# A decoder trunk on one core: the last expert's down products follow the ones ahead in two pieces, and a branch gets a hint

## The chip, the core and the metric

The kernel runs on one core of a Trainium2 chip. TensorE (PE in the profile) multiplies, VectorE (DVE) and ScalarE (ACT) work element by element, GpSimd (POOL) does a little beside them, and SyncE (SP) issues the loads. The metric is the device time of one execution in microseconds, the median of three runs. A trace of one further execution shows when every instruction ran.

## The reference

Two decoder layers over 256 tokens of width 1024, in float32. Layer 0 mixes with a retention, layer 1 with a sparse attention whose keys and values come from the stream after layer 0. Both end with the same kind of mixture of experts, which is all that the change touches:

```python
for l in range(DEPTH):                       # 2 layers
    mix = retention(...) if l < 1 else nsa_attention(...)
    h = layer_norm(ALPHA * h + mix, ...)
    h = layer_norm(ALPHA * h + moe(h, ...), ...)

def moe(x, ...):                             # 256 tokens, 16 experts in 4 groups, each token has 2
    y = zeros_like(x)
    for e in range(16):
        he = (silu(x @ w_gate[e]) * (x @ w_up[e])) @ w_down[e]   # 1024 -> 512 -> 1024
        y = y + w[:, e:e + 1] * he
    return y
```

## The kernel before

Each expert takes up to 64 tokens: a gather by a one-hot product writes them into a tile `xT` (three buffers, two experts in each), and all products of the expert run on these 64 rows. If some expert has more than 64 tokens, a loop behind a branch (`overflow`, L880) does the rest; with these inputs it isn't entered, and all engines jump past it. Every engine loads the largest count from memory, compares and branches. On the way past it the engine adds to its own counter what the loop would have added, once its work ahead is done; engines that wait for such a counter wait for that.

TensorE's work for expert e stands in this order. `gate_up(e + 1)` makes 16 product pairs from 64 rows; in the middle of it, behind the fourth weight step, stand the transposes of expert e (`turn`, L804), the scatter of expert e - 1 (L825, four products of 128x512 into the sums `y_moe`) and other small pieces. Then `down(e)` makes the 64x512 products of expert e into two PSUM banks, one for each half of the 1024 outputs, on two halves of TensorE's columns (`both`, L776). Between them stand the other engines: `hidden` takes the bank of `gate_up` to the rows `sh` (ScalarE's Silu at L795, VectorE's multiplication at L796), `turn` goes from `sh` over a bank to `hT` (ScalarE, L805), and `hilo` takes the banks of `down` to `out` as a rounded high part (ScalarE, L222) and the rest (VectorE, L223). For the last expert there is no `gate_up` to hide this in: transposes, scatter of expert 14, `down(15)` and scatter of expert 15 follow each other.

The weights come in chunks of 1 MB through a ring, loaded by SyncE in their order; an expert has six (four for gate and up, two for down). The expert weights are used as they are. The dense weights that come behind layer 0's experts are split first, by half chunks, into a high part (ScalarE, L114) and a low part (VectorE, L115), into four places `st`. `Weights.ahead` splits as far as places and a limit allow; `get` gives the next half chunk and lets go of those before, `take` lets go of none. Before, two half chunks are split at expert 14 and two at expert 15 of layer 0 (`split_ahead`). The order of all instructions is that of the code, engine by engine; the framework adds the waits.

Behind the experts come the statistics of the sums (L306), and the normalisation, in layer 0 (`next_rows`) into transposed columns `hTh` and `hTl` (L1020, L1026), in layer 1 (`last_rows`) into the output.

Of the kernel before, what the change touches and what calls it, by code (L numbers as in the profile page):

```python
# [10 lines left out]
F32 = mybir.dt.float32  # L11
F32R = mybir.dt.float32r
# [7 lines left out]
P = 128  # L20
# [3 lines left out]
NE = 16  # L24
# [129 lines left out]
class Trunk:  # L154
# [46 lines left out]
    def alloc(self, name, side="right"):  # L201

        self.extra.append(self.tc.alloc_tile_pool(name=name, bufs=1, side=side, reuse_waits="tile"))
        return self.extra[-1]

    def split_ahead(self, n):

        self.W.limit = 2 * self.moe_end(0) + n
        self.W.ahead()

    def first_place(self, l, side):

# [501 lines left out]
    def experts(self, pool, keep, oh0, rest, hh, hl, y, l):  # L714
# [4 lines left out]
        out = []  # L719
# [31 lines left out]
        def weigh(g):  # L751

            b = self.bank()
            for i in range(4):
                for tb in range(2):
                    nc.tensor.matmul(b[0:64, i:i + 1], oh[g][:, tb, i, :].bitcast(F32),
                                     self.w[:, tb, 4 * g + i:4 * g + i + 1], start=(tb == 0), stop=(tb == 1))
            ws[g] = pool.tile([P, 4], F32, tag="wsl", name=f"wsl{l}_{g}", bufs=2)
            nc.vector.tensor_copy(ws[g][0:64], b[0:64, 0:4])
# [12 lines left out]
        def both(x, w, b, first, last, o=0):  # L772

            for i in range(2):
                c = slice(64 * i ^ o, (64 * i ^ o) + 64)
                nc.tensor.matmul(b[i][c, :], x, w[:, i, :], start=first, stop=last)  # L776

        def gate_up(e, fill, at=3):


            b = self.bank()
            for k in range(8):
                both(xT[e // 2][:, e % 2, k, :], self.W.get(2)[0], [b, b], k == 0, k == 7, 64)
                if k == at:
                    for f in fill:
                        f()
            return b
# [10 lines left out]
        def hidden(e, b):  # L798
            gated(b, ws[e // 4][0:64, e % 4:e % 4 + 1])

        def turn(hT):
            b = self.bank()
            for k in range(4):
                nc.tensor.transpose(b[:, k * P:k * P + P], rows[:, k * P:k * P + P], self.ident)  # L804
            nc.scalar.copy(hT, b.rearrange("p (k s) -> p k s", k=4)[:, :, 0:64])  # L805

        def down(e, hT):

            b = [self.bank(), self.bank()]
            for k in range(4):  # L810
                both(hT[:, k, :], self.W.get(2)[0], b, k == 0, k == 3)
            if not out:
                out.append(self.first.tile([P, 2048], F32R, tag="raw", name=f"out{l}"))
            d = []
            for i in range(2):
                t = out[0][:, i * 512:i * 512 + 512]
                hi, lo = t[64 * i:64 * i + 64], t[64 - 64 * i:128 - 64 * i]
                self.hilo(hi, lo, b[i][64 * i:64 * i + 64, :])
                d.append(t)
            return d  # L820

        def scatter(e, d, last):

            o = oT[e // 4][:, e % 2, e % 4 // 2]
            return [lambda tb=tb, nh=nh: nc.tensor.matmul(y[tb][nh], o[:, tb, :], d[nh], start=(e == 0), stop=last)  # L825
                    for nh in range(2) for tb in range(2)]
# [40 lines left out]
        def overflow():  # L867
# [8 lines left out]
            d = part[0:64, 256:512]  # L876
            pe = pool.tile([P, 2, 2], F32, name=f"o_pe{l}")
            wsl = pool.tile([P, 1], F32, name=f"o_ws{l}")
            most = nc.values_load(self.cnt[0:1, 0:1], min_val=0, max_val=2 * P)
            with self.tc.If(most > 64), self.tc.For_i(0, NE, 1) as e:  # L880
                nc.vector.tensor_copy(pe[:, 0, :], self.pos[:, :, ds(e, 1)])
                nc.vector.tensor_copy(pe[:, 1, :], self.w[:, :, ds(e, 1)])

# [45 lines left out]
        hidden(0, b)  # L929
        d = self.gb = None  # L930
        picks, todo, more = [], [], alpha()
        for e in range(NE):
            g = e // 4 + 1
            if e % 4 == 1 and g < 4:
                oh[g] = self.one_hot(keep, g, l)
                picks = gather(g)
            hT = pool.tile([P, 4, 64], F32, tag="hT", name=f"hT{l}_{e}", bufs=1)
            fill = [lambda: turn(hT)] + (scatter(e - 1, d, False) if e else [])
            if e % 4 == 0 and e:
                fill.append(lambda: turn_hot(e // 4))  # L940
            if e + 1 < NE:
                fill += more[:1] + picks[:2] + todo[:2]
                more, picks, todo = more[1:], picks[2:], todo[2:]
                b = gate_up(e + 1, fill)
                if e % 4 == 2 and g < 4:
                    weigh(g)
                hidden(e + 1, b)
            else:
                for f in fill:
                    f()  # L950
            if e == 13:
                overflow()
            if l == 0 and e >= NE - 2:
                self.split_ahead(2 * (e - NE + 3))
            d = down(e, hT)
            if e == 0:
                turn_hot(0)
            if l == 1 and e > 9 and self.gb is None and self.W.slots:
                todo += norm_rows()
        for f in todo:  # L960
            f()
        self.ready(AF.Sqrt)
        for f in scatter(NE - 1, d, True):
            f()
        self.W.limit = 2 * len(self.W.srcs)

# [607 lines left out]
```

## Time and profile before

| what | value |
|---|---|
| median of 3 runs | 890.33 us (889.71 to 890.62) |
| the profiled execution | 891.96 us, its span 890.10 us |
| TensorE busy | 846.9 us, 95% of the span |
| VectorE, ScalarE busy | 405.6 us, 339.7 us |
| 1024 gate and up products 128x512 (L776) | 233.9 us busy |
| 512 down products 128x512 (L776) | 118.6 us busy |
| branches in the executed path | 2, one in each layer, at L880 |

TensorE is busy in nearly every slice of the span. A matmul of the code on float32 data is two in the trace, so `down` has sixteen and `gate_up` thirty-two; two run at a time on the two halves of the columns. In a timeline row, "x16" are sixteen instructions merged, and what stands in brackets is the idle time of that engine ahead of the row and what ended it.

### The profile page before, as it was taken

The page shows a single profiled execution, that of the slowest core. Times are in us where ns is not written, and L with a number is a line of the kernel's source. Part 1 is how long each engine was busy: PE and PEld are TensorE (multiplying, and loading weights), DVE is VectorE, ACT ScalarE, POOL GpSimd, SP SyncE. Part 2 cuts the span into 40 slices and gives each one's busy share as a digit, 9 for nine tenths or more (in the row PEclk, how much of TensorE's full clock was granted, in tenths as well). Part 3 has the DMA queues.
Part 4 walks back from the last instruction along what each step waited for, and adds up shares of the span by engine and source line. Part 5 has one row for each costly group of instructions (what it writes and reads, how often), then busy time and mean ns, then how long its engine had stood idle before and what let it go on. Part 6 is the DMA issues. An engine that isn't in the chain of part 4 may idle for free. (4 is left out here: it accounts for less than half of the span.)

```text
span 890.1 us, 12109 instructions
## 1 busy us (share of the span) xinstructions
PE 846.9 (95%) x4738; PEld 535.0 (60%) x4738; DVE 405.6 (46%) x817; ACT 339.7 (38%) x657; POOL 50.0 (6%) x70
## 2 busy tenths in 40 slices
PE   7999999998999999999879998999999999999993
PEld 5998989886545454453338786666744545445431
DVE  4666776864422132221077877775433222222215
ACT  4335344434332331322164455785523233232312
POOL 1000000000200000000000004220110000000001
PEclk8999999999999999999999999899999999999997
DMA  9966354578699999999943456205779999999801
GB/s 332 426 248 231 119 218 142 190 279 350 224 409 410 426 423 427 422 425 423 365 156 138 169 230 237 96 1 203 308 280 388 425 427 424 427 426 427 375 3 47
DMA packets 37283, 259.83 MB, mean 292 GB/s; under 512 B 4217, under 2 KB 4401, under 8 KB 6369
## 3 DMA queue, kind: packets, MB, share of 16 engines
q1 hardware_dynamic: 36432, 255.87, 71.3%
q0 software_dynamic: 640, 2.97, 1.0%
q8 instruction: 42, 0.69, 0.3%
q14 instruction: 25, 0.20, 0.1%
q10 hardware_dynamic: 144, 0.11, 0.0%
HBM read 257.88 MB, written 1.05 MB: 291 GB/s over the span
## 5 line engine op out<-in xcount | busy, mean ns | idle before, releaser
L776 PE MATMUL bank<-raw,xT 128*64 128x512 f32 x1024 | 233.9, 596 | 0.8 <-ACT xT L735 0.8
L776 PEld LDWEIGHTS bank<-raw,xT 128*64 128x64 f32 x1024 | 76.7, 137 | 125.9 <-issue 118.5
L115 DVE TENSOR_TENSOR st<-raw,st 128x1024 fp32r<-128x1024 f32 x92 | 111.4, 1234 | 55.4 <-ACT st L114 55.3
L114 ACT CAST st<-raw 128x1024 fp32r<-128x1024 f32 x92 | 94.5, 1048 | 80.4 <-PE bank L339 32.4
L776 PE MATMUL bank<-raw,hT 128*64 128x512 f32 x512 | 118.6, 601 | 5.2 <-PEq L880 3.3
L323 PE MATMUL bank<-xh,st 128*128 128x256 f32 x512 | 93.6, 284 | 3.0 <-ACT st L114 2.5
L223 DVE TENSOR_TENSOR out<-bank,out 64x512 fp32r<-64x512 f32 x64 | 44.1, 689 | 96.7 <-ACT out L222 95.6
L776 PEld LDWEIGHTS bank<-raw,hT 128*64 128x64 f32 x512 | 40.5, 138 | 73.3 <-issue 70.1
L323 PEld LDWEIGHTS bank<-xh,st 128*128 128x128 f32 x512 | 80.4, 192 | 3.6 <-ACT st L114 2.7
L222 ACT CAST out<-bank 64x512 fp32r<-64x512 f32 x64 | 37.1, 579 | 104.6 <-PE bank L776 103.8
L323 PE MATMUL bank<-xl,st 128*128 128x256 f32 x256 | 72.3, 283 | 0.0
L796 DVE SCALAR_TENSOR_TENSOR sh<-bank,wsl,sh 64x512 f32<-64x512 f32 x32 | 23.7, 741 | 105.3 <-ACT sh L795 105.1
L795 ACT ACTIVATE sh<-bank 64x512 f32<-64x512 f32 x32 | 19.0, 593 | 94.9 <-PE bank L776 94.9
L323 PEld LDWEIGHTS bank<-xl,st 128*128 128x128 f32 x256 | 49.6, 194 | 0.1
L805 ACT COPY hT<-bank 128x256 f32<-128x256 f32 x32 | 11.9, 373 | 86.9 <-PE bank L804 86.9
L356 PE MATMUL acc<-st,gh 128*128 128x512 f32 x128 | 42.9, 407 | 1.8 <-DVE st L115 1.1
L339 PE MATMUL bank<-st,hTh 128*128 128x512 f32 x128 | 42.2, 401 | 1.7 <-DVE nt L1022 1.4
L825 PE MATMUL y_moe<-out 128*128 128x512 f32 x128 | 38.6, 419 | 4.4 <-DVE out L223 4.4
L840 DVE SCALAR_TENSOR_TENSOR al<-bank,wsm,al 128x256 f32<-128x256 f32 x16 | 7.7, 484 | 72.0 <-ACT al L839 72.0
L339 PE MATMUL bank<-st,xh 128*128 128x512 f32 x128 | 40.5, 393 | 0.0
L733 DVE TENSOR_SCALAR xT<-bank,wsm 128x128 f32<-128x128 f32 x64 | 21.9, 404 | 34.0 <-PE bank L727 24.2
L735 ACT ACTIVATE xT<-bank,wsm 128x128 f32<-128x128 f32 x64 | 24.1, 456 | 19.3 <-PE bank L727 19.3
(328 smaller groups left out, 1205.4 us busy)
## 6 DMA issues: line engine op xcount, KB each, us to landing
raw<-in_w_moe_dram SPq DMA_DIRECT2D x190, 1024.0 KB, 10.3
raw<-in_w_dense_dram SPq DMA_DIRECT2D x49, 1024.0 KB, 7.0
raw<-in_w_moe_dram SPq DMA_DIRECT2D x4, 512.0 KB, 15.6
xT<-in_x_T_dram SPq DMA_DIRECT2D x4, 256.0 KB, 5.4
raw<-in_w_dense_dram SPq DMA_DIRECT2D x2, 512.0 KB, 10.0
rt<-in_c_ret_dram POOLq DMA_DIRECT2D x1, 1024.0 KB, 11.1
gb<-in_ln_rows_dram POOLq DMA_DIRECT2D x1, 1024.0 KB, 6.9
out_dram<-lf_n SPq DMA_DIRECT2D x4, 256.0 KB, 2.0
```

What stands on the lines that cost most here:

```text
L114: self.nc.scalar.copy(hi, r)
L115: (eng or self.nc.vector).tensor_sub(lo, r, hi.bitcast(F32))
L222: self.nc.scalar.copy(hi, src)
L223: self.nc.vector.tensor_sub(lo, src, hi.bitcast(F32))
L323: self.nc.tensor.matmul(b[:, m, :], w[:, kk, c], x[:, k, :], start=(k == 0 and i == 0 and m == 0), stop=(k == 7 and i == 2 and m == 1))
L339: self.nc.tensor.matmul(b[tb], x[:, k, c], w[:, kk, :], start=(k == 0 and i == 0), stop=(k == 7 and i == 2))
L356: self.nc.tensor.matmul(y[tb][nh], x[a][:, c], w[b][:, 0, n], start=False, stop=last and i == 2)
L733: nc.vector.tensor_scalar(t, v, c, d, op0=ALU.mult, op1=ALU.add)
L735: nc.scalar.activation(t, v, AF.Identity, bias=d, scale=c)
L776: nc.tensor.matmul(b[i][c, :], x, w[:, i, :], start=first, stop=last)
L796: nc.vector.scalar_tensor_tensor(rows[0:64], b[0:64], w, rows[0:64], op0=ALU.mult, op1=ALU.mult)
L825: return [lambda tb=tb, nh=nh: nc.tensor.matmul(y[tb][nh], o[:, tb, :], d[nh], start=(e == 0), stop=last) for nh in range(2) for tb in ran ...
```

## The change

There are three parts. (1) `down` gets the tile that it writes, a number of pieces, and work that is put behind its second weight step. At expert 14 that work is expert 15's `turn`, into a tile of its own (`hT_last`, in a buffer of `xT`). Expert 15's `down` then follows expert 14's at once, in two pieces of 256 of the 512 columns of each bank, with its own result tile `d_last`, and both scatters stand behind it. (2) `mark_branch_hint_location` puts one hint instruction into TensorE's stream, for the branch past the overflow. (3) Layer 0's splits ahead move: three half chunks at expert 13, just behind the branch, in place of two at expert 14 and two at expert 15; the fourth follows in `next_rows`, at a call of `ahead` that was there before.

```diff
-    def split_ahead(self, n):
-
-        self.W.limit = 2 * self.moe_end(0) + n
-        self.W.ahead()
...
-        def down(e, hT):
+        def down(hT, t, parts=1, fill=()):
+
 
             b = [self.bank(), self.bank()]
-            for k in range(4):
-                both(hT[:, k, :], self.W.get(2)[0], b, k == 0, k == 3)
...
+            ws = []
+            n = 512 // parts
+            for p in range(parts):
+                c = slice(p * n, p * n + n)
+                for k in range(4):
+                    if k == 2 and p == 0:
+                        for f in fill:
+                            f()
+                    if p == 0:
+                        ws.append(self.W.take(2)[0] if k and parts > 1 else self.W.get(2)[0])
+                    both(hT[:, k, :], ws[k][:, :, c], [v[:, c] for v in b], k == 0, k == 3)
+                for i in range(2):
+                    v = t[:, i * 512 + c.start:i * 512 + c.stop]
+                    self.hilo(v[64 * i:64 * i + 64], v[64 - 64 * i:128 - 64 * i], b[i][64 * i:64 * i + 64, c])
+            return [t[:, i * 512:i * 512 + 512] for i in range(2)]
...
+            self.tc.mark_branch_hint_location(f"past{l}", "LikelyTaken", engines=(mybir.EngineType.PE,))
             most = nc.values_load(self.cnt[0:1, 0:1], min_val=0, max_val=2 * P)
-            with self.tc.If(most > 64), self.tc.For_i(0, NE, 1) as e:
+            with self.tc.If(most > 64, label=f"past{l}"), self.tc.For_i(0, NE, 1) as e:
...
-        for e in range(NE):
+        spare = lambda dtype, name: pool.tile([P, 1024], dtype, tag="xT", name=f"{name}{l}", bufs=3)
+        for e in range(NE - 1):
...
             if e == 13:
                 overflow()
-            if l == 0 and e >= NE - 2:
-                self.split_ahead(2 * (e - NE + 3))
-            d = down(e, hT)
+                if l == 0:
+
+                    self.W.limit = 2 * self.moe_end(0) + 3
+                    self.W.ahead()
...
+            between = []
+            if e == NE - 2:
+
+                last = spare(F32, "hT_last")[:, 0:256].rearrange("p (k s) -> p k s", k=4)
+                between.append(lambda: turn(last))
+            d = down(hT, out[0], 1, between)
...
+        d_last = down(last, spare(F32R, "d_last"), 2)
+        for f in scatter(NE - 2, d, False):
+            f()
         self.ready(AF.Sqrt)
-        for f in scatter(NE - 1, d, True):
+        for f in scatter(NE - 1, d_last, True):
             f()
```

The lines of the changed kernel have other numbers: `both` is L771, `turn` L799, `hilo` L217 and L218, the branch L881. On TensorE, at the end of layer 1's experts, this stood before (`bank375` and `bank376` take expert 14's products, `bank378` and `bank379` expert 15's, `raw239` and `raw240` are weight chunks; in brackets the engines whose counters the row waits for):

```order
L776 MATMUL bank376_7346<-raw239_6855,hT1_14_7311 64x512
L804 MATMUL bank377_7360<-cst_105,sh1_5762 128x128 [waits DVE_49]
L804 MATMUL bank377_7360<-cst_105,sh1_5762 128x128 x3
L825 MATMUL y_moe1_00_5752<-out1_5925 128x512 [waits DVE_49]
L825 MATMUL y_moe1_10_5754<-out1_5925 128x512
L825 MATMUL y_moe1_01_5753<-out1_5925 128x512 [waits DVE_49]
L825 MATMUL y_moe1_11_5755<-out1_5925 128x512
L776 MATMUL bank378_7370<-raw240_6861,hT1_15_7359 64x512 [waits DMAHW7_49,Activation_49]
L776 MATMUL bank379_7371<-raw240_6861,hT1_15_7359 64x512 [waits PE_49]
L776 MATMUL bank378_7370<-raw240_6861,hT1_15_7359 64x512
```

With the change, from the last of expert 14's products on, it reads:

```order
L771 MATMUL bank376_7362<-raw239_6869,hT1_14_7326 64x512
L771 MATMUL bank378_7382<-raw240_6875,hT_last1_7360 64x256 [waits DMAHW7_49,Activation_49]
L771 MATMUL bank379_7383<-raw240_6875,hT_last1_7360 64x256 [waits PE_49]
L771 MATMUL bank378_7382<-raw240_6875,hT_last1_7360 64x256
L771 MATMUL bank379_7383<-raw240_6875,hT_last1_7360 64x256
L771 MATMUL bank378_7382<-raw241_6906,hT_last1_7360 64x256 [waits DMAHW0_49]
L771 MATMUL bank379_7383<-raw241_6906,hT_last1_7360 64x256
L771 MATMUL bank378_7382<-raw241_6906,hT_last1_7360 64x256 [waits DMAHW1_49]
L771 MATMUL bank379_7383<-raw241_6906,hT_last1_7360 64x256
L771 MATMUL bank378_7382<-raw240_6875,hT_last1_7360 64x256 [waits DVE_49]
L771 MATMUL bank379_7383<-raw240_6875,hT_last1_7360 64x256 [waits DVE_49]
L771 MATMUL bank378_7382<-raw240_6875,hT_last1_7360 64x256
```

Expert 15's products now follow expert 14's; the transposes into `bank377` went up between the two halves of expert 14's products, and both scatters stand behind the second piece, which begins at the two rows that wait for VectorE. Layer 0 has the same order.

On ScalarE, just behind layer 0's branch (the first row), this stood before (`st256` to `st259` are split half chunks of the dense chunks `raw128` and `raw129`; `bank162` and `bank163` hold expert 13's products):

```order
L880 UNCONDITIONAL_BRANCH x2
L222 CAST out0_2353<-bank162_3711 64x512
L222 CAST out0_2353<-bank163_3712 64x512
L805 COPY hT0_14_3729<-bank165_3743 128x256
L795 ACTIVATE sh0_2194<-bank164_3730 64x512
L114 CAST st256_3763<-raw128_3339 128x1024
L114 CAST st257_3766<-raw128_3339 128x1024
L222 CAST out0_2353<-bank166_3769 64x512
L222 CAST out0_2353<-bank167_3770 64x512
L805 COPY hT0_15_3783<-bank168_3784 128x256
L114 CAST st258_3794<-raw129_3355 128x1024
L114 CAST st259_3797<-raw129_3355 128x1024
```

and with the change:

```order
L881 UNCONDITIONAL_BRANCH x2
L114 CAST st256_3712<-raw128_3339 128x1024
L114 CAST st257_3715<-raw128_3339 128x1024
L114 CAST st258_3718<-raw129_3355 128x1024
L217 CAST out0_2341<-bank162_3721 64x512
L217 CAST out0_2341<-bank163_3722 64x512
L800 COPY hT0_14_3739<-bank165_3753 128x256
L790 ACTIVATE sh0_2194<-bank164_3740 64x512
L800 COPY hT_last0_3773<-bank168_3780 128x256
L217 CAST out0_2341<-bank166_3774 64x512
L217 CAST out0_2341<-bank167_3775 64x512
L217 CAST d_last0_3794<-bank169_3795 64x256
```

Three casts went ahead of expert 13's, and no split is left between the casts of the last experts; VectorE's subtractions moved alike. On TensorE the hint for layer 0's branch is the second instruction of the program, and that for layer 1's stands where the loop's code has been passed in layer 0, ahead of expert 13's down products:

```order
L881 COMPARE_AND_BRANCH
L881 UNCONDITIONAL_BRANCH x2
L1581 BRANCH_PREFETCH_HINT
L771 MATMUL bank162_3721<-raw118_3184,hT0_13_3333 64x512
L771 MATMUL bank163_3722<-raw118_3184,hT0_13_3333 64x512
```

The hint is new there; the rows around it stood so before.

## Rows read from the trace of the kernel before

**Rows 1.** Timeline of TensorE's products around layer 0's branch: start, length, instructions, [idle before]

```profile
424.40 3.65 PE L776 MATMUL bank<-raw,xT 128*64 128x512 f32 x16
...
431.33 4.89 PE L776 MATMUL bank<-raw,hT 128*64 128x512 f32 x13 [3.27 <-PEq L880]
436.41 0.65 PE L776 MATMUL bank<-raw,hT 128*64 128x512 f32 x2 [0.20 <-issue]
436.84 0.59 PE L776 MATMUL bank<-raw,xT 128*64 128x512 f32 x1
```

**Rows 2.** Instructions of the branch, layer 0: ns min/median/max, first and last start

```profile
L880 PEldq COMPARE_BRANCH  x1: 5888/5888/5888, 425.0 to 425.0; - x1
...
L880 DVEq EVENT_SEMAPHORE  x1: 21/21/21, 430.0 to 430.0; - x1
```

**Rows 3.** Stretches: length, busy time of each engine, granted clock, DMA share, GB/s

```profile
431.54:434.96 3.42, 3.42 (x10) 1.21 (x8) 0.00 (x0) 0.00 (x0) 0.59 (x2) 0.50 0.85 350
...
552.21:555.13 2.92, 0.00 (x1) 0.01 (x2) 2.78 (x6) 1.06 (x5) 2.84 (x4) 0.88 0.55 233
555.20:558.00 2.80, 2.80 (x12) 1.72 (x12) 2.77 (x8) 2.35 (x7) 2.65 (x4) 0.50 0.00 0
...
851.92:855.40 3.48, 3.48 (x17) 1.43 (x19) 0.00 (x0) 0.00 (x0) 0.00 (x0) 1.00 0.00 0
```

**Rows 4.** Instructions of the branch, layer 1

```profile
L880 PEldq COMPARE_BRANCH  x1: 3632/3632/3632, 847.0 to 847.0; - x1
...
L880 DVEq EVENT_SEMAPHORE  x1: 21/21/21, 851.7 to 851.7; - x1
```

**Rows 5.** Timeline of all engines, first products behind layer 1's branch

```profile
851.92 3.65 PE L776 MATMUL bank<-raw,hT 128*64 128x512 f32 x16 [1.73 <-DVEq L880]
```

**Rows 6.** Timeline of TensorE at the end of layer 1's experts

```profile
865.00 3.60 PE L776 MATMUL bank<-raw,hT 128*64 128x512 f32 x16
868.53 0.66 PE L804 MATMUL bank<-cst,sh 128*128 128x128 f32 x4
869.99 1.46 PE L825 MATMUL y_moe<-out 128*128 128x512 f32 x4 [0.80 <-DVE out L223]
871.37 3.65 PE L776 MATMUL bank<-raw,hT 128*64 128x512 f32 x16
876.41 1.46 PE L825 MATMUL y_moe<-out 128*128 128x512 f32 x4 [1.38 <-DVE out L223]
```

**Rows 7.** Timeline of TensorE at the end of layer 0's experts

```profile
445.85 3.60 PE L776 MATMUL bank<-raw,hT 128*64 128x512 f32 x16
...
457.26 1.46 PE L825 MATMUL y_moe<-out 128*128 128x512 f32 x4 [1.38 <-DVE out L223]
```

**Rows 8.** Timeline of VectorE at the end of layer 1's experts

```profile
865.84 0.74 DVE L796 SCALAR_TENSOR_TENSOR sh<-bank,wsl,sh 64x512 f32<-64x512 f32 x1 [8.24 <-ACT sh L795]
...
875.67 1.41 DVE L223 TENSOR_TENSOR out<-bank,out 64x512 fp32r<-64x512 f32 x2 [5.01 <-ACT out L222]
877.11 1.89 DVE L306 BATCH_NORM_STATS2 lf_st<-y_moe 128x6 f32<-128x512 f32 x3
```

**Rows 9.** Timeline of all engines among layer 0's experts

```profile
384.49 0.37 ACT L805 COPY hT<-bank 128x256 f32<-128x256 f32 x1 [2.89 <-PE bank L804]
...
385.16 0.40 PE L727 MATMUL bank<-oh,hh 128*128 128x256 f32 x2
...
386.80 0.40 PE L727 MATMUL bank<-oh,hl0l 128*128 128x256 f32 x2
...
390.62 0.98 PE L756 MATMUL bank<-w,oh 128*64 128x1 f32 x15
```

**Rows 10.** Groups on VectorE, 452 to 480: busy us, mean ns | idle

```profile
L115 DVE TENSOR_TENSOR st<-raw,st 128x1024 fp32r<-128x1024 f32 x5 | 6.0, 1223 | 2.7 <-ACT st L114 2.7
...
L1026 DVE TENSOR_TENSOR hTl<-nt,hTh 128x256 fp32r<-128x256 f32 x2 | 0.9, 426 | 0.1
```

**Rows 11.** The one load of a dense chunk issued at 423.0: time to landing

```profile
DMA to landing us min/median/max: 8.3/8.3/8.3
```

More of the change, by code (lines that the diff above doesn't have):

```diff
@@ L805, in turn @@
             nc.scalar.copy(hT, b.rearrange("p (k s) -> p k s", k=4)[:, :, 0:64])
-        def down(e, hT):
+        def down(hT, t, parts=1, fill=()):
             b = [self.bank(), self.bank()]
-            for k in range(4):
-                both(hT[:, k, :], self.W.get(2)[0], b, k == 0, k == 3)
[L812 to L820, printed above, removed]
+            ws = []
[13 more added lines that the diff above has]
+            return [t[:, i * 512:i * 512 + 512] for i in range(2)]
         def scatter(e, d, last):
@@ L942, in experts @@
                 fill += more[:1] + picks[:2] + todo[:2]
[L943 to L950, printed above, removed]
+            more, picks, todo = more[1:], picks[2:], todo[2:]
+            b = gate_up(e + 1, fill)
+            if e % 4 == 2 and g < 4:
+                weigh(g)
+            hidden(e + 1, b)
             if e == 13:
                 overflow()
-            if l == 0 and e >= NE - 2:
-                self.split_ahead(2 * (e - NE + 3))
-            d = down(e, hT)
+                if l == 0:
+                    self.W.limit = 2 * self.moe_end(0) + 3
+                    self.W.ahead()
+            if e == 0:
+                out.append(self.first.tile([P, 2048], F32R, tag="raw", name=f"out{l}"))
+            between = []
[3 more added lines that the diff above has]
+            d = down(hT, out[0], 1, between)
             if e == 0:
```

## The prediction

> **What bounds the kernel now.** I read the page first, then the waits at the branch, then the last expert of each layer, since the diff touches nothing else. TensorE is busy nearly throughout, so only stretches where it stands still or runs at half clock can give time back. The reader is to see three of them, all on TensorE, all on the path because the engines around it have nothing else to finish.
>
> First, the branch around the overflow in layer 0. The products of expert 14's gate and up end at 424.40 + 3.65 = 428.05, and the first product behind the branch starts at 431.33 [rows 1]: 3.27 us idle, put down to TensorE's own branch. That branch stood 5.89 us in TensorE's sequencer, from 425.0 to 430.9, while VectorE had posted its count at 430.0 [rows 2]. TensorE needs that count, since VectorE makes the rows `sh` just ahead of its own branch. Behind the wait come slow products: 16 of them take from 431.33 to 436.84, 5.51 us [rows 1], where the same 16 in layer 1 take 851.92 to 855.38. The granted clock was 0.50 (1.2 GHz) from 431.54 to 434.96 [rows 3], which makes 1.7 us of the 2.05 lost; the rest is a stop that the row at 436.41 calls "issue" [rows 1].
>
> Second, the same branch in layer 1. TensorE's branch took 3.63 us from 847.0, so it was through at 850.6, and VectorE's count came only at 851.7 [rows 4]; the products start at 851.92 after 1.73 us, released by VectorE [rows 5]. The clock stayed at 1.00 behind it [rows 3].
>
> Third, the end of each layer's experts. From the start of expert 14's down products (865.00) to the first scatter of expert 15 (876.41) it takes 11.41 us [rows 6], the same in layer 0 (445.85 to 457.26) [rows 7]. In it TensorE idles 0.80 us until VectorE has the low part of expert 14, and 1.38 us until it has that of expert 15 [rows 6].
>
> **The tail, worked out.** Write T for 865.00. The products come in pairs, sixteen in about 3.43 us. Expert 15's transposes move between the two halves of expert 14's down products: they want `sh`, which VectorE finishes at 865.84 + 0.74, T + 1.58 [rows 8], and TensorE gets there at T + 1.8, so they wait for nothing. Four transposes hold TensorE about 0.42 us beside their drain [rows 6], so expert 15's products can start at S = T + 4.0 instead of T + 6.37. ScalarE copies `hT_last` (0.37 us [rows 9]) long before.
>
> The first piece is sixteen products of 256 columns. No row has that shape in half-width tiles. At half of 3.43 it is 1.72 us; at the pace of the 128x256 gather products, two each 0.235 us (385.16 to 386.80 is seven such steps [rows 9]), 1.88 us. I take 1.72 and keep 1.88.
>
> Now the point that the diff hides: the second piece's first two products carry a wait on VectorE each, since both pieces lie in the same two PSUM banks. The pieces do not overlap with their own evacuation. The results of piece one can be read at S + 1.93. ScalarE's cast of 64x256 costs near the 0.37 of a 128x256 copy; VectorE's subtraction 0.42, as the 128x256 one of 426 ns [rows 10], where 64x512 takes 0.69 (1.41 for two [rows 8]). Bank one: cast until S + 2.33, subtraction until S + 2.78. Bank two: subtraction until S + 3.21. With 0.06 us to TensorE the second piece runs in full from S + 3.27, to S + 4.99. Expert 14's scatter, put behind it, takes some 1.1 us and covers the last casts (0.16 + 0.37 + 0.42 and three handovers, S + 6.06). Expert 15's scatter so starts at S + 6.1 = T + 10.1, against T + 11.41: 1.3 us less. The bank statistics start 0.70 us behind it now, at 877.11, because VectorE is still at L223 until 877.07 [rows 8]; then it is free, which gives another 0.1. So 1.4 us per layer, 2.8 us in all. Bounds: with 1.88 us pieces 1.1; with the subtraction at the full 0.69 as well 0.4; nothing above 1.5. The activation table load moves with the last cast and is done well before the square root.
>
> **The branch hint.** It is one instruction at the start of the block, per layer; ahead of the first products and inside a wait it costs nothing. If the code behind the branch is there when TensorE arrives, layer 0 is held by VectorE's count as layer 1 is: 430.0 + 0.22 (851.7 to 851.92) is 430.2, so 1.1 us less. The stop of 0.34 us at 436.4 should be more code that arrives late, since TensorE comes to the target 5 us earlier; I take 0.3 (0 to 0.34). The half clock I leave: idle falls from 3.27 to 2.2 us; 1.73 us left the clock at 1.00 in layer 1 [rows 3, 5], 2.92 us ahead of 555.13 left it at 0.50 [rows 3]; 2.2 lies between. Layer 1 gains nothing: there VectorE is later than the branch already.
>
> The Trainium skill, Runtime: NRT & Kernel Launch, section "Instruction fetch mechanics", says that a taken branch out of the fetched pages forces a DMA fetch, and that prefetch is purely sequential. The rows of 5.89 and 3.63 us agree with the first. By the second the hint would change nothing, and the sum would be the tail's 2.8 us alone; no row here shows a hinted branch.
>
> **Three half chunks split ahead.** In layer 0 three casts and three subtractions (1.22 us each on VectorE [rows 10], and I take no more for a cast) move from the tail to just behind the branch, ahead of expert 13's casts in ScalarE's and VectorE's queues. What stands behind them there are those casts and the scatter of expert 13, which waits for them. The third needs the second dense chunk, which is issued at 423.0 and lands 8.3 us later, at 431.3 [rows 11], so ScalarE is through by 432.5 and VectorE by 433.8; expert 13's products end at 433.7 at the earliest, and VectorE's turn comes only behind a cast. Cost nothing; cover gone only if the chunk lands later than 433. The fourth half chunk goes into the normalisation of layer 0, between the third and last pair of transposed columns: bounded by 0 and one 1.22 us step; I take 0, as 36 products of the same projection come before its first use. SP's next loads (the ring place of the first dense chunk) start earlier by some 2 us and one later chunk starts later; the ring stays ahead. The tail has no split left in ScalarE's queue, but its split casts cost nothing there before either.
>
> **Rivals.** *B, the clock comes back too:* with 2.2 us idle the stretch at 0.50 may not come; 1.7 us more. For it: 1.73 us did no harm. Against it: 2.92 us did. 890.33 - 5.9 = 884.4. *C, the hint does nothing:* TensorE's prefetch takes no notice or the target is displaced in the 400 us between hint and branch. For it: the hint stands far ahead, and the rule above. Against it: nothing in the rows. 890.33 - 2.8 = 887.5. *D, slower:* products of 256 columns pay the price of 512, because each brings its own weight load; 32 loads instead of 16 in expert 15's down products. Then each layer loses 3.43 and gains 1.4: with the hint 890.33 + 4.1 - 1.4 = 893.0. It turns the whole slower once one such product occupies more than 0.173 us (2 x (1.4 - 32 x (s - 0.107)) + 1.4 = 0). Against it: fifteen products of one column with their 64-wide loads go through in 0.98 us, 0.065 each [rows 9], and the gather's 256 columns go at 0.117. *E, no change to speak of:* no hint effect and VectorE's half subtraction as long as the whole one: 0.4 per layer, 889.5.
>
> **How the numbers follow.** The sum is 2.8 + 1.1 + 0.3 = 4.2 us. The profiled execution took 891.96 (span 890.10 and 1.86 around it), 1.63 over the median 890.33; I take the difference from the median: 886.1. Chances: this forecast (A) 0.40, B 0.19, C 0.25, D 0.06, E 0.10. The range reaches from B with the tail at its upper bound (884.0) to C with 1.0 per layer (888.4), and holds A, B and nearly all of C. Within 0.2% is 1.8 us to either side, about what a measurement of this kernel can tell from no change: A, B and C are faster (0.84), E is the same (0.10), D slower (0.06).
>
> **What would show it.** In the new trace: TensorE's branch in layer 0 under 1 us, the idle before expert 13's down products near 2.2 us and released by VectorE; in layer 1 still 1.7. From expert 14's down products to expert 15's scatter 10.0 us in both layers, with an idle of about 1 us between the two pieces, released by VectorE at the split line. It is wrong if the second piece starts without that wait (then 1.2 us more per layer), if the branch still takes 5 us, or if products of 256 columns come less than twice as often as those of 512.

## The result

The changed kernel takes 885.47 us (median of 17 runs, 882.87 to 888.73) where the kernel before took 890.62 on the same chip (17 runs, 888.96 to 894.12): 0.9938 of the time, 95% interval 0.9926 to 0.9951, or 4.4 to 6.6 us less. The forecast said 886.1, within 884.0 to 888.4. Of the experiments below, one run of e2 (1239.2 us at a mean granted clock of 0.648) and one of e4 (903.5 us at 0.933) stand far above the others of their kernel, and the medians and ratios leave them out.

The profiled execution of the changed kernel took 886.01 us (span 884.0). The first thing to look at is TensorE at the branch in layer 0 (start, length, then the work, and in brackets the idle time before it; [rows 1] before):

```profile
424.61 3.65 PE L771 MATMUL bank<-raw,xT 128*64 128x512 f32 x16
430.43 3.65 PE L771 MATMUL bank<-raw,hT 128*64 128x512 f32 x16 [2.17 <-ACT st L114]
433.88 3.63 PE L771 MATMUL bank<-raw,xT 128*64 128x512 f32 x16
```

Three things have gone: 1.10 us of the idle time (3.27 to 2.17), the slow pace of the sixteen products behind it (3.45 us to the next ones, where 5.51 passed before), and the stop that cut them in two at 436.41. The stop cost more than its 0.20 us of idle time, because it left the products behind it out of step: the last of the sixteen ran beside the first of expert 15's gate products, and the transposes behind those came only at 440.85 (TensorE, before):

```profile
436.90 0.59 PE L776 MATMUL bank<-raw,hT 128*64 128x512 f32 x1
437.27 3.65 PE L776 MATMUL bank<-raw,xT 128*64 128x512 f32 x15
440.85 0.66 PE L804 MATMUL bank<-cst,sh 128*128 128x128 f32 x4
```

From the first of the sixteen to these transposes it took 9.52 us; now it takes 7.01 (430.43 to 437.44). The releaser in the bracket is the profile's guess. The instructions of the branch in this stretch show the real one ([rows 2] before):

```profile
L881 PEldq COMPARE_BRANCH  x1: 388/388/388, 425.2 to 425.2; - x1
...
L881 DVEq COMPARE_BRANCH  x1: 72/72/72, 429.6 to 429.6; - x1
L881 DVEq EVENT_SEMAPHORE  x1: 21/21/21, 430.2 to 430.2; - x1
```

TensorE's branch took 0.39 us instead of 5.89, and what is waited for now is VectorE's count at 430.2, with the products 0.2 us behind it. In layer 1 the branch fell from 3.63 to 0.35 us and nothing came of it, since VectorE's count was the later one there already ([rows 4, 5] before):

```profile
L881 PEldq COMPARE_BRANCH  x1: 350/350/350, 842.2 to 842.2; - x1
...
L881 DVEq EVENT_SEMAPHORE  x1: 21/21/21, 846.8 to 846.8; - x1
```

```profile
847.11 3.65 PE L771 MATMUL bank<-raw,hT 128*64 128x512 f32 x16 [1.73 <-DVEq L881]
```

The second thing is the granted clock, in the row of stretches (length; busy time of the engines; clock; DMA share; GB/s). Before, most of the products behind the branch ran at 0.50 [rows 3]; now, over the idle time and over the products:

```profile
428.26:430.43 2.17, 0.01 (x2) 0.03 (x1) 0.81 (x2) 1.86 (x3) 0.11 (x1) 1.00 1.02 408
430.43:433.88 3.45, 3.45 (x16) 1.40 (x18) 3.45 (x3) 1.78 (x2) 0.90 (x2) 1.00 1.01 399
```

The third is the end of layer 0's experts ([rows 7] before, and [rows 6] for the same in layer 1). TensorE:

```profile
442.45 1.89 PE L771 MATMUL bank<-raw,hT 128*64 128x512 f32 x8
444.26 0.66 PE L799 MATMUL bank<-cst,sh 128*128 128x128 f32 x4
444.85 1.94 PE L771 MATMUL bank<-raw,hT 128*64 128x512 f32 x8
446.62 1.90 PE L771 MATMUL bank<-raw,hT_last 128*64 128x256 f32 x16
449.41 2.40 PE L771 MATMUL bank<-raw,hT_last 128*64 128x256 f32 x16 [0.90 <-DVE d_last L218]
451.74 1.20 PE L825 MATMUL y_moe<-out 128*128 128x512 f32 x4
452.78 1.08 PE L825 MATMUL y_moe<-d_last,out 128*128 128x512 f32 x4
```

and VectorE ([rows 8] before):

```profile
448.94 0.87 DVE L218 TENSOR_TENSOR d_last<-bank,d_last 64x256 fp32r<-64x256 f32 x2
451.83 0.88 DVE L218 TENSOR_TENSOR d_last<-bank,d_last 64x256 fp32r<-64x256 f32 x2 [2.02 <-ACT d_last L217]
453.28 1.89 DVE L301 BATCH_NORM_STATS2 lf_st<-y_moe 128x6 f32<-128x512 f32 x3 [0.57 <-PE y_moe L825]
```

Expert 15's scatter starts 10.33 us behind expert 14's products (11.41 before), and the statistics 0.50 us behind the scatter (0.70 before). The only idle time left on TensorE is 0.90 us between the two pieces, and VectorE's first pair of subtractions is what ends it.

Over the whole profile: from expert 14's gate products to the first product of the next stage, layer 0 takes 29.09 us instead of 34.16 (5.07 less). In layer 1 it is 28.78 instead of 29.87 from there to expert 15's scatter, and 13.44 instead of 13.69 from the scatter to the end (1.34 less). The start of the kernel is 0.21 longer and the 388 us between the two 0.05 longer, which gives the 6.15 us between the spans, 890.10 and 883.95.

### The profile page after: what moved, and what is told of

Read it like the earlier page. It is cut to its first block, busy times and chain, and to the rows that moved or that the text cites. A ratio compares the mean times of both kernels' runs of the same rounds, so it can differ in the third digit from the quotient of the medians.

```text
span 884.0 us, 12189 instructions
## 1 busy us (share of the span) xinstructions
PE 844.7 (96%) x4770; PEld 536.9 (61%) x4770; DVE 405.7 (46%) x821; ACT 340.8 (39%) x661; POOL 49.5 (6%) x70
## 5 line engine op out<-in xcount | busy, mean ns | idle before, releaser
L771 PE MATMUL bank<-raw,xT 128*64 128x512 f32 x1024 | 233.5, 596 | 0.8 <-ACT xT L730 0.8
L771 PEld LDWEIGHTS bank<-raw,xT 128*64 128x64 f32 x1024 | 76.6, 137 | 125.9 <-issue 118.7
L771 PE MATMUL bank<-raw,hT 128*64 128x512 f32 x480 | 109.4, 594 | 3.9 <-ACT st L114 2.2
L218 DVE TENSOR_TENSOR out<-bank,out 64x512 fp32r<-64x512 f32 x60 | 41.3, 688 | 86.1 <-ACT out L217 85.2
L771 PEld LDWEIGHTS bank<-raw,hT 128*64 128x64 f32 x480 | 37.5, 137 | 65.4 <-issue 59.8
L217 ACT CAST out<-bank 64x512 fp32r<-64x512 f32 x60 | 34.8, 580 | 89.0 <-PE bank L771 88.2
L825 PE MATMUL y_moe<-out 128*128 128x512 f32 x120 | 35.2, 415 | 0.0
## 6 DMA issues: line engine op xcount, KB each, us to landing
raw<-in_w_moe_dram SPq DMA_DIRECT2D x190, 1024.0 KB, 10.1
```

The source lines that it names most:

```text
L217: self.nc.scalar.copy(hi, src)
L218: self.nc.vector.tensor_sub(lo, src, hi.bitcast(F32))
```

## The experiments

Each kernel was timed beside the kernel before on the same chip, where that took 890.5 to 891.2 us (medians). Ratios are to those runs, with 95% intervals; between kernels of different chips they are the fairer comparison. "L0" in the table is the time from the start of expert 14's gate products to the first product of the next stage in layer 0, "L1" that to the start of expert 15's scatter in layer 1, both read off TensorE's timeline of the profiled execution; "idle" is TensorE's idle time at the two branches, "16 products" the length of those behind layer 0's branch ("slow, cut": partly at half clock, and interrupted by a stop).

| kernel | L0 | L1 | idle | 16 products | median us | ratio |
|---|---|---|---|---|---|---|
| before | 34.16 | 29.87 | 3.27, 1.73 | slow, cut | 890.6 | 1 |
| changed | 29.09 | 28.78 | 2.17, 1.73 | 3.65 | 885.5 | 0.9938 [0.9926, 0.9951] |
| e1 no hint | 32.81 | 28.79 | 3.25, 1.73 | slow, cut | 889.4 | 0.9986 [0.9971, 1.0001] |
| e2 hint only | 30.55 | 29.86 | 2.16, 1.73 | 3.65 | 885.6 | 0.9944 [0.9926, 0.9961] |
| e3 one piece | 28.29 | 27.61 | 2.16, 1.73 | 3.65 | 882.5 | 0.9908 [0.9888, 0.9928] |
| e4 own banks | 28.12 | 27.80 | 2.17, 1.73 | 3.65 | 882.1 | 0.9911 [0.9889, 0.9934] |
| e5 splits back | 35.69 | 28.78 | 2.17, 1.73 | 5.35 | 888.0 | 0.9964 [0.9949, 0.9979] |
| e9 late count | 31.49 | 29.92 | 2.85, 2.85 | 5.35 | 889.4 | 0.9984 [0.9968, 0.9999] |
| e12 hint for VectorE too | 29.12 | 28.78 | 2.20, 1.73 | 3.65 | 888.4 | 0.9973 [0.9956, 0.9991] |
| e6 early branch | 27.59 | 27.60 | 0.51, 0.41 | 3.80 | 879.0 | 0.9875 [0.9853, 0.9898] |
| e7 early, own banks | 26.55 | 26.68 | 0.51, 0.41 | 3.75 | 879.1 | 0.9861 [0.9839, 0.9884] |
| e8 early, one piece | 26.73 | 26.38 | 0.51, 0.41 | 3.75 | 881.6 | 0.9899 [0.9881, 0.9918] |
| e10, the same again | 26.78 | 26.39 | 0.51, 0.42 | 3.79 | 879.9 | 0.9874 [0.9852, 0.9896] |
| e11 early, no hint | 33.09 | 27.92 | 3.47, 0.78 | slow, cut | 886.3 | 0.9949 [0.9932, 0.9965] |

**The two parts apart.** e1 takes the hint out of the changed kernel, e2 puts it alone into the kernel before:

```diff
-            self.tc.mark_branch_hint_location(f"past{l}", "LikelyTaken", engines=(mybir.EngineType.PE,))
-            with self.tc.If(most > 64, label=f"past{l}"), ...
+            with self.tc.If(most > 64), ...
```

> The changed kernel without the branch hint (last expert's two pieces and the early splits stay). Theory, the parts add and the hint is worth what layer 0 shows: TensorE's branch takes about 5.9 us again in layer 0 and 3.6 in layer 1, the idle before expert 13's down products in layer 0 is 3.3 us instead of 2.17, the clock falls to half behind it, and the time is 2.6 us below the kernel before (888.0), which is 1.1 to 3.2 us above the changed kernel. Rival, the time fell through the last expert alone and the hint only moved a wait: no more than 0.5 us above the changed kernel (885.5 to 886).

> The kernel before with nothing but the hint. Theory: branch 0.4 us in both layers, idle 2.2 us in layer 0 and 1.7 as before in layer 1, no gain in layer 1; 1.4 us off without the clock, 3.1 with it, so 887.5 to 889.2. Rival, VectorE's count is what binds in both layers, and the gain is the 1.1 us alone: 889.5, with the slow products still behind the wait.

TensorE behind layer 0's branch in e1, without the hint:

```profile
430.15 4.89 PE L771 MATMUL bank<-raw,hT 128*64 128x512 f32 x13 [3.25 <-ACT st L114]
435.37 0.65 PE L771 MATMUL bank<-raw,hT 128*64 128x512 f32 x2 [0.33 <-issue]
```

and in e2, with nothing but the hint:

```profile
426.20 3.65 PE L776 MATMUL bank<-raw,xT 128*64 128x512 f32 x16
432.02 3.65 PE L776 MATMUL bank<-raw,hT 128*64 128x512 f32 x16 [2.16 <-DVEq L881]
```

The branches are as the theory of each expectation had them. The stages add: the tail gives 1.35 us in layer 0 (34.16 to 32.81), the hint 3.61 (34.16 to 30.55), both 5.07. So the hint, which the forecast valued at 1.4 us, carries most of the result. The runs divide it less evenly, and neither time is the one expected: by the ratios e2 is 5.0 us under the kernel before (interval 3.5 to 6.6; 1.4 to 3.1 expected) and e1 1.2 under it (-0.1 to 2.6; 2.6 expected), where the stages give the hint 3.6 and the tail 2.7 in both layers. No run explains the difference.

The profile pages show that the hint also spares transfers of instructions (packets, MB, share of time). There were 42 packets in every kernel without it, the kernel before among them, and 40 in every kernel with it, as in the changed one: two fewer, and there are two branches. What those two carried is not shown.

```profile
q8 instruction: 42, 0.69, 0.3%
...
q8 instruction: 40, 0.66, 0.3%
```

**Are the two pieces worth it?** e3 makes expert 15's down products in one piece, e4 gives the second piece two banks of its own:

```diff
-        d_last = down(last, spare(F32R, "d_last"), 2)
+        d_last = down(last, spare(F32R, "d_last"), 1)
```

```diff
             for p in range(parts):
+                if p:
+                    b = [self.bank(), self.bank()]
```

> The changed kernel with the last expert's down products in one piece of 512 columns. Theory, the two pieces only meet their own evacuation in the same PSUM banks: without them the idle of 0.90 us between the pieces is gone, expert 14's scatter starts 1.2 us earlier in both layers, VectorE's last subtraction ends 0.4 us earlier, and the time is 0.4 to 0.6 us per layer below the changed kernel, 1.0 in all (884.5). Rival, the smaller pieces are worth their wait because the last cast and subtraction are half as long: expert 15's scatter starts 0.3 us later in each layer, the time 0.6 us above the changed kernel.

> The changed kernel, with the second piece in two PSUM banks of its own (those of expert 14's products). Theory, the idle between the pieces is the wait for the evacuation of the first: it falls from 0.90 us to about 0.3 (VectorE's last subtraction of expert 14), and expert 15's scatter starts 0.55 us earlier in both layers, the time 1.1 us below the changed kernel. Rival, VectorE is the bound there anyway: the pieces move together, the subtractions queue behind each other, and the scatter starts within 0.1 us of where it did.

TensorE at the end of layer 0 in e3:

```profile
445.43 3.60 PE L771 MATMUL bank<-raw,hT_last 128*64 128x512 f32 x16
448.96 1.19 PE L825 MATMUL y_moe<-out 128*128 128x512 f32 x4
450.42 1.46 PE L825 MATMUL y_moe<-d_last,out 128*128 128x512 f32 x4 [0.26 <-DVE d_last L218]
451.72 3.43 PE L247 MATMUL bank<-bits 128*128 128x384 bf16 x20
```

and in e4:

```profile
447.23 4.22 PE L771 MATMUL bank<-raw,hT_last 128*64 128x256 f32 x32
451.37 1.20 PE L827 MATMUL y_moe<-out 128*128 128x512 f32 x4
452.41 1.09 PE L827 MATMUL y_moe<-d_last,out 128*128 128x512 f32 x4
```

Both are shorter than the changed kernel. e3 is 0.80 us shorter in layer 0. In layer 1 its scatter comes 1.17 earlier, but the rest up to the end takes 13.71 instead of 13.44, so 0.90 is left. e4 is 0.97 shorter in layer 0 and 0.98 in layer 1. With banks of its own the second piece follows the first without idle time (32 products in one row; a weight load in it waits until 449.50 for VectorE's last subtraction of expert 14, behind products that are still running): the 0.90 us was the evacuation of the same two banks, as the forecast had put it. What the forecast did not ask is whether the pieces are worth that wait; they are not. Both gains are larger than expected (1.0 and 1.1 us). The runs (2.7 and 2.4 us under the changed kernel by the ratios) go further than the stages' 1.7 and 1.95, by no more than the intervals allow.

**The splits.** e5 puts the half chunks back where they stood, two ahead of expert 14's and two ahead of expert 15's down products:

```diff
-                if l == 0:
-                    self.W.limit = 2 * self.moe_end(0) + 3
-                    self.W.ahead()
...
+            if l == 0 and e == NE - 2:
+                self.W.limit = 2 * self.moe_end(0) + 2
+                self.W.ahead()
             d = down(hT, out[0], 1, between)
...
+        if l == 0:
+            self.W.limit = 2 * self.moe_end(0) + 4
+            self.W.ahead()
         d_last = down(last, spare(F32R, "d_last"), 2)
```

> The changed kernel with the half chunks split where the kernel before split them (two ahead of expert 14's down products, two ahead of expert 15's; none behind the branch). Theory: splits cost nothing in either place, stages of layer 0 within 0.1 us of the changed kernel's and the time within 1 us of it. Rival, with expert 15's products straight on, the splits in ScalarE's and VectorE's queues hold up the last casts: a cast and a subtraction of 1.2 us each stand ahead of expert 14's and 15's evacuation, and the end of layer 0's experts comes 1 to 2 us later.

TensorE, between the two pieces:

```profile
449.12 1.90 PE L771 MATMUL bank<-raw,hT_last 128*64 128x256 f32 x16
454.48 4.13 PE L771 MATMUL bank<-raw,hT_last 128*64 128x256 f32 x16 [3.45 <-DVE d_last L218]
458.54 1.81 PE L825 MATMUL y_moe<-out 128*128 128x512 f32 x4
```

VectorE over the same time, and the granted clock of two stretches:

```profile
451.61 2.36 DVE L115 TENSOR_TENSOR st<-raw,st 128x1024 fp32r<-128x1024 f32 x2 [0.27 <-ACT st L114]
454.00 0.88 DVE L218 TENSOR_TENSOR d_last<-bank,d_last 64x256 fp32r<-64x256 f32 x2
```

```profile
432.59:436.00 3.41, 3.41 (x12) 1.18 (x10) 0.00 (x0) 0.00 (x0) 0.00 (x0) 0.50 1.01 394
...
453.07:459.90 6.83, 5.42 (x19) 3.28 (x20) 2.59 (x5) 1.84 (x4) 0.00 (x0) 0.50 0.87 323
```

The rival was right, and its 1 to 2 us were too few. With expert 15's products straight on, two splits stand ahead of the casts that the second piece waits for: the idle time grows by 2.55 us, the clock falls to half, and the products and the scatter behind it take 1.73 and 0.61 longer. That is 4.9 us in layer 0; the other 1.7 of the 6.6 in the table are the products behind the branch, which in this execution ran at half clock after the same idle time as in the changed kernel. This execution was the slowest of e5's ten (892.28 us); the median is 2.5 us above the changed kernel's, about what the idle time alone gives. Behind the branch the splits cost nothing: idle time and products there are the same in e2, which has none in that place (2.16 and 3.65 us).

**What the clock answers to.** e9 leaves the hint in and delays VectorE's count, by a reduction of 128x1024 between `sh` and the branch:

```diff
             if e == 13:
+                slack = pool.tile([P, 1], F32, name=f"slack{l}")
+                nc.vector.tensor_reduce(slack, xT[7].rearrange("p a k s -> p (a k s)"), axis=AX.X, op=ALU.add)
                 overflow()
```

> The changed kernel with one extra VectorE reduction of 128x1024 (about 1.1 us) between `sh` of expert 14 and the branch, in both layers, so that VectorE's count comes later while the hint stays. Theory, the slow products behind layer 0's branch were the clock's answer to the idle time: layer 0's idle grows to 3.3 us, the half clock is back behind it with 1.7 us of slow products and no further stop; layer 1's idle grows to 2.8, near the 2.9 us that another pause of this kernel has with half clock behind it; 3.9 to 5.6 us above the changed kernel. Rival, the slow products came from the unhinted branch itself (code arriving late): the products behind both branches stay at full pace and only the waits grow, 2.2 us above.

Stretches of e9: the idle time and the half clock behind it in layer 0, the idle time and the products behind it in layer 1. Below them stands TensorE behind layer 0's branch.

```profile
428.18:431.03 2.85, 0.00 (x0) 0.03 (x1) 1.94 (x3) 2.54 (x3) 0.11 (x1) 1.00 1.01 417
432.23:435.64 3.41, 3.41 (x10) 1.19 (x8) 2.23 (x2) 0.10 (x1) 0.00 (x0) 0.50 0.90 346
...
847.67:850.52 2.85, 0.00 (x0) 0.03 (x1) 1.87 (x2) 0.59 (x1) 0.00 (x0) 1.00 0.01 3
850.52:853.98 3.46, 3.46 (x17) 1.41 (x19) 0.00 (x0) 0.00 (x0) 0.00 (x0) 1.00 0.02 5
```

```profile
431.03 5.35 PE L771 MATMUL bank<-raw,hT 128*64 128x512 f32 x16 [2.85 <-DVEq L881]
...
439.75 0.66 PE L799 MATMUL bank<-cst,sh 128*128 128x128 f32 x4
```

In layer 0 the half clock is back with the hint in place, and the sixteen products take 5.35 us in one row, without a stop. From the first of them to the transposes it takes 8.72 us, between the 9.52 of the kernel before and the 7.01 of the changed kernel. So the slow pace belongs to the clock (1.7 us) and the stop at 436.41 to the missing hint (0.8 us): it shows behind layer 0's branch in the three kernels without one (idle time of 0.20, 0.33 and, in e11, 0.38 us) and in none with it, at either clock. With the 1.1 us of idle time these are the 3.61 of the hint. Behind layer 1's branch no kernel shows a stop. The theory held in layer 0 only: the same 2.85 us left the clock at 1.00 in layer 1, so the length of the pause alone does not decide. Over the profiles, layer 0's branch was followed by half clock after 3.27, 3.25, 3.47 and 2.85 us, after 2.16 to 2.20 us once in six, and never after 0.51.

**The branch ahead of `sh`.** e6 moves expert 14's activation and product behind the branch. The code under the branch gets three banks of its own, since the products' bank is still full when it is reached:

```diff
             b = gate_up(e + 1, fill)
...
-            hidden(e + 1, b)
             if e == 13:
                 overflow()
+            hidden(e + 1, b)
+            if e == 13:
                 if l == 0:
...
+            ring = itertools.cycle([self.bank() for _ in range(3)])
+            self.bank = lambda: next(ring)
             most = nc.values_load(self.cnt[0:1, 0:1], min_val=0, max_val=2 * P)
```

e7 adds e4's banks to it, e8 and e10 e3's single piece, and e11 takes the hint out of e6.

> The changed kernel with the branch ahead of expert 14's activation and product on ScalarE and VectorE (they follow it instead of standing ahead of it; the branch's own code takes three banks of its own for that). Theory, what is left at the branch in both layers (2.17 and 1.73 us) is TensorE waiting for VectorE's count behind `sh`: both fall under 0.3 us, the time 3.3 to 3.9 us below the changed kernel (881.8). Rival, TensorE's own branch needs that time or the code behind it arrives then: the idle stays over 1 us and a stop shows among the products behind it, less than 2 us gained.

> Early branch, and the second piece of expert 15's products in two banks of its own. The stage from expert 14's gate products to the next stage of layer 0 took 29.09 us in the changed kernel, 27.59 with the early branch, 28.12 with own banks; if the two add, 26.6 us here and 26.6 from expert 14's gate products to expert 15's scatter in layer 1 (28.78, 27.60, 27.80). The time then is 1.8 to 2.0 us below the early branch alone: 877 to 878. Rival, the half-clock stretches elsewhere differ between runs by more than that and hide it: the stages add but the median lies within 2 us of 879.0.

> Early branch as in the run before it and expert 15's down products in one piece of 512 columns. Theory, the two gains add: 3.6 us from the branch and 0.9 (layer 0: 29.09 to 28.29 us from expert 14's gate products to the next stage's first product) and about 1 in layer 1, 5.5 us below the changed kernel: 880. Rival, they overlap, since expert 14's `sh` now comes later behind the branch and delays its transposes: 1 us less.

> The same program as the early branch with one piece, timed anew beside the others. If its 881.6 us against 879.0 for the early branch alone came of the half-clock stretches (its stages were 0.9 and 1.2 us shorter), its median falls to 877 to 879 here; if something in it costs time that the stages at the branch do not show, it stays at 881 or more.

> Early branch without the hint. Theory, TensorE's own branch of 5.9 and 3.6 us is then the one that binds: idle 2.9 us in layer 0 (branch from 425.0 to 430.9, gate products done at 428.0) with the clock often at half behind it, and 0.6 to 0.8 us in layer 1; 3 to 5 us above the early branch with the hint, 883. Rival, the branch came so late only because of the waits around it: idle near 0.5 us as with the hint, time 879.

The branch in layer 0 of e6, and TensorE's products around it:

```profile
L884 DVEq EVENT_SEMAPHORE  x1: 21/21/21, 421.9 to 421.9; - x1
...
L884 PEldq COMPARE_BRANCH  x1: 388/388/388, 424.9 to 424.9; - x1
...
L884 PEldq EVENT_SEMAPHORE  x1: 51/51/51, 428.0 to 428.0; - x1
```

```profile
424.33 3.65 PE L772 MATMUL bank<-raw,xT 128*64 128x512 f32 x16
428.49 3.80 PE L772 MATMUL bank<-raw,hT 128*64 128x512 f32 x16 [0.51 <-PEq L884]
```

and in e11, without the hint:

```profile
L883 PEldq COMPARE_BRANCH  x1: 6088/6088/6088, 426.2 to 426.2; - x1
```

```profile
432.72 4.89 PE L772 MATMUL bank<-raw,hT 128*64 128x512 f32 x13 [3.47 <-PEq L883]
```

VectorE's count now comes 6 us before TensorE is through in layer 0, and the idle time falls to 0.51 and 0.41 us, more than the 0.3 expected: TensorE posts its own count only once its products are done (428.0), and starts 0.5 us behind that. e6 takes 5.6 us off the changed kernel by the ratios where the stages give 2.7 and 3.3 to 3.9 were expected. Its mean granted clock was 0.988 over six runs, the changed kernel's 0.983 over seventeen, so part of the rest is clock elsewhere, which no run here explains. Without the hint the early branch gives nothing in layer 0 (33.09 us, 32.81 in e1): TensorE's branch takes 6.09 us there and binds alone, with half clock behind it. The median of e11 is 7 us above e6's, where 3 to 5 were expected.

The stages add in e7, e8 and e10 (26.4 to 26.8 us in both layers, about 2 us below e6), but the medians do not follow: 879.1, 881.6 and 879.9, with mean clocks of 0.985, 0.983 and 0.984. e8 and e10 are one program, 1.7 us apart, and e10 lies between its two expectations. The four early kernels with the hint are 9 to 12 us faster than the kernel before; which of them is best, these runs do not settle.

**VectorE's own branch.** e12 gives the hint to VectorE too:

```diff
-... engines=(mybir.EngineType.PE,))
+... engines=(mybir.EngineType.PE, mybir.EngineType.DVE))
```

> The changed kernel with the same hint for VectorE as well. Layer 0's idle is 2.17 us where layer 1's is 1.73; VectorE's count follows its branch by 0.6 us in layer 0 and 0.3 in layer 1. Theory, the 0.3 us are VectorE's own code behind the branch: with the hint its count follows after 0.3 us in both layers or less, idle 1.8 in layer 0, time 0.3 us less, which the comparison can't show but the profile can. Rival, its code is there and the count waits for its own last product: unchanged at 0.6 and 0.3.

VectorE's branch and its count, first start in layer 0, last in layer 1:

```profile
L881 DVEq COMPARE_BRANCH  x2: 74/79/84, 429.9 to 846.7; - x2
L881 DVEq EVENT_SEMAPHORE  x2: 21/21/21, 430.5 to 847.1; - x2
```

The count follows after 0.6 and 0.4 us as before: nothing gained there, and the rival stands so far that the code was not late. The stages are the changed kernel's, yet the runs are about 3 us slower; the last section says where that lies.

## Why the prediction came out right, point by point

- **Where the time was.** Right: the three stretches named give 6.4 us, the two spans differ by 6.15.
- **The tail, 1.4 us per layer.** Right in size: 1.35 in layer 0 (e1 against before) and 1.34 in layer 1. Step by step: expert 15's products start at T + 4.17 (T + 4.0 predicted), because the four transposes hold TensorE from 444.26 to 444.85, 0.59 us where 0.42 was taken, and the second half of expert 14's products starts at T + 2.40. The first results are read at S + 1.92 (1.93), the subtractions take 0.43 each (0.42), the second piece runs in full from S + 3.25 (3.27; the weight load of its second product waits until 449.87), and expert 15's scatter comes at S + 6.16 (6.1). Of the 0.23 between the 10.1 forecast and 10.33, 0.17 is this start. The statistics gained 0.2 instead of 0.1.
- **Products of 256 columns.** Right: sixteen take a row of 1.90 us, of which the last product is 0.38, so the eight pairs start 0.217 us apart and take 1.73 us, the 1.72 that was taken. It is half of what 512 columns take (3.60 and 0.59, so 0.43 from pair to pair). Rival D is out.
- **The hint, 1.1 + 0.3 us in layer 0 and 0 in layer 1.** Right in mechanism: branch 0.39 us, idle time 2.17, released by VectorE's count, the stop gone, layer 1 unchanged at 1.73. The 1.1 is right; the 0.3 for the stop is too small, and so is its bound of 0.34. The forecast read the rows only up to the next product at 436.84, and the products behind that were still out of step: with them the stop cost 0.8 us. Rival C is out by e2. The Trainium skill, "Runtime: NRT & Kernel Launch", section "Instruction fetch mechanics", calls prefetch purely sequential, by which the hint would do nothing; the branch of 5.89 us that became 0.39 disagrees, and the measurement decides.
- **The clock left at half: the term that was most mis-sized.** The step "2.2 lies between" took the cautious side, and the profile of the changed kernel took the other: 1.00 behind 2.17 us, so rival B's 1.7 us came on top. The hint was worth 3.61 us in layer 0 (1.1, 0.8 and 1.7), not 1.4. It is no certain gain: e5 had the half clock after the same 2.17 us. The median lies between the forecast (4.2 us less) and B (5.9 less), at 5.15 less. That it came within 0.7 us of the forecast is in part luck: the two profiles differ by 6.15 us, and in how many of the runs the half clock stayed away is not shown. The lower end of the range, B with 1.5 us per layer, adds up to 884.2 and not 884.0.
- **The splits at nothing: right only as far as it went.** "Its split casts cost nothing there before either" is true of the kernel before, where expert 15's products came late anyway. It does not carry over to a tail in which they come early: left there, they cost 4.9 us of layer 0 in e5's profile, half clock included, and 2.5 us of the median. The sum was right because the tail was worked out as if they were gone; moving them is a condition of the tail's gain, not a part at no cost.
- **What was not asked.** Whether each piece of the change earns its place. One piece, or two in banks of their own, is 0.8 to 1.0 us per layer better than the change as made.

## What to carry to other kernels

Look at a taken branch in the queue of its own engine. If it stands there for microseconds, a hint can remove that (here 5.89 us became 0.39), and the gain goes only as far as the next thing waited for, here another engine's count that comes early enough once the branch is moved ahead of two instructions. Before work is cut into pieces, ask whether the pieces share a bank: if they do, the second waits for the evacuation of the first, and one long piece may end earlier. A step that costs nothing where it stands may cost microseconds once the work around it moves up, so price it in the new order.

## What the hardware showed beyond that

- The granted clock behind a pause is not a function of the pause's length: 2.17 us with 1.00 in the changed kernel and 0.50 in e5; 2.85 us with 0.50 in layer 0 and 1.00 in layer 1 of one execution of e9. Elsewhere too half-clock stretches come and go between kernels that are the same there (between 204 and 234 us e1 and e3 have none, the changed kernel has two). The runs follow them: of the changed kernel's seventeen the two slowest (888.6 and 888.7 us) had a mean clock of 0.979, the three fastest (882.9 to 883.5) 0.986 to 0.988. What decides it stays open.
- An unhinted taken branch of TensorE is dear and unequal: 5.87 to 6.09 us in layer 0, 3.41 to 3.63 in layer 1 (the kernel before, e1 and e11), against 0.39 and 0.35 with the hint in all profiles. VectorE's branch takes 0.06 to 0.07 us without a hint, and its count follows the branch's start after 0.2 to 0.6 (later only in e9, with its extra reduction).
- A hint for a second engine cost time outside the span: e12's runs stand 4.65 us above their spans, the changed kernel's 2.04 (medians of the differences), those of every other kernel here 1.8 to 2.3. The profile shows nothing of it, and its cause was not looked for.
